# An encoder trunk in fp32 on one core: latents copied out of their banks, squares taken chunk by chunk, taps booked by the number of chunks under way, a warm-up activation in the join

## The chip, the core and the metric

The kernel runs on one core of a Trainium2 chip. The metric is the device time of one execution in microseconds: 1187.85 us, the median of three runs (1186.94 to 1188.17). The profiled execution took 1188.38 us.

## What is computed

A two-layer encoder on x of 512 positions and 1024 channels, in float32. Each sub-layer is `x = x + rms_norm(f(rms_norm(x)))`.

```python
def parallel_conv_mla(h, ...):        # layer 0
    proj = h @ w_in                   # gates and input of a 3-tap convolution, q_lat (384), kv_lat (256), k_rope
    y_a = gate_b * depthwise_conv(gate_c * xs, sc_kernel)
    q = rms_norm(q_lat, q_norm) @ w_uq
    kv = rms_norm(kv_lat, kv_norm) @ w_ukv
    ...
    y_b = block_attention(q_full, k_full, v)
    return jnp.concatenate([y_a, y_b], axis=-1) @ w_out

def conformer_conv(h, ...):           # layer 1
    u = h @ w_pw1 + b_pw1
    a, g = jnp.split(u, 2, axis=-1)
    u = a * jax.nn.sigmoid(g)
    u = depthwise_conv(u, w_dw) + b_dw          # 31 taps per channel
    u = jax.nn.silu(layer_norm(u, ln_g, ln_b))
    return u @ w_pw2 + b_pw2

def squared_relu_mlp(h, w1, w2):      # both layers, hidden width 4096
    return jnp.square(jax.nn.relu(h @ w1)) @ w2
```

## The kernel before

Everything is held transposed: channels in eight chunks of 128 partitions, positions along the free axis. A float32 product is made of three matmuls on pairs of a high and a low part (`mm`, L242 to L248). `strip` (L210) loads a strip of weights of 128 x 1024, lets ACT round it to the high part (`whi`, L223) and GpSimd subtract to the low part (`wlo`, L224); `split` (L227) does the same for activations, on ACT (L230) and mostly on VectorE (L233, L236, L238). So one strip is 24 matmuls in one PSUM bank. The eight banks are named by use: S (three), pj (two), mi (two) and o (one). `scratch` (L174) takes o and mi in turn, and under a norm or join also pj.

The start (L557 to L609). `split_x` loads a chunk of x, multiplies it by its gain into a scratch bank (L569) and splits it into a pair h. `START` says between which chunks the first two strips of `win` are loaded. After all eight chunks, each is squared (`Sum.square`, L357, into a scratch bank) and added up on VectorE (`Sum.add`, L332). `Sum.done` adds over partitions with small matmuls (L367), `rstd` works out 1/sqrt on VectorE in some twelve small instructions (L390 to L425), and `spread` brings the result back to all partitions with matmuls (L432). ACT copies it out as R0 (L595). `latent` (L598) makes five latents, each a strip's product, multiplied by R0 in its own bank (L603), squared for its norm, and split from there.

The second part (`M2`, L36) is a program written out by hand: steps of the two halves A and B of the positions. While the chain of one half runs (a norm, a join), `hold` and `pace` pull steps of the other half in (`step`, L293), until the next step of the same half or the next chain. The 31 taps of the convolution run on VectorE (`convolve`, L813; L827), each adding into the chunk's bank in place. Chunks stand in `convs` as generators; `fill(us)` (L276) adds us to a credit after every matmul step and issues taps of the first two chunks in turn as long as the credit covers the cost of a tap, which is `TAP_US` by the width of the half. `norm_step` (L927) first issues the taps that are left, pulling a step for each `STEP_US - OP_US` of them, and then runs `layer_norm`, which ends in the pairs h that `pw2` multiplies. `up_step` (L885) lets ACT take the square of the relu as long as taps are left, and VectorE after that.

VectorE's order in this part is the order of the code. The other engines' order, and all orders of the first part, are set by a scheduler at build time, which may place an instruction wherever its operands are ready. `warm` is a 1-element tile on which an activation is called only to have a function's table loaded (L847, silu).

Of the kernel before, what the change touches and what calls it, by code (L numbers as in the profile page):

```python
# [12 lines left out]
AF = mybir.ActivationFunctionType  # L13
# [4 lines left out]
T = 512  # L18
# [18 lines left out]
M3 = [('up', 'B', 1, 3, 0, 8), ('down', 'B', 1, 3, 0, 8), ('finish', 'B')]  # L37


OP_US, STEP_US = 0.39, 2.35  # L40
TAP_US = {T // 2 - PAD: 0.41, T // 2 + PAD: 0.44}
FILL = {'up': 2.3, 'down': 2.3, 'first': 2.6, 'sum': 1.8, 'pw1': 4.8, 'pw2': 2.3}
START = ['x', (128,), 'x', (256, 512, 768), 'x', 'x', 'x', 'x', 'x', 'x', ()]
ADD0 = 0
# [87 lines left out]
def trunk(ctx: ExitStack, tc: tile.TileContext, a, out: bass.AP):  # L132
# [11 lines left out]
    def new(pool, tag, bufs, w=T, dt=F32):  # L144
        uid[0] += 1
        return pool.tile([P, w], dt, tag=tag, bufs=bufs, name=f"{tag}{uid[0]}")
# [46 lines left out]
    def small(w=NB):  # L193
        return new(sp, f"s{w}", 8 if w == 1 else 12, w)
# [77 lines left out]
    def settle(keep=0):  # L272
        while len(late) > keep:
            late.pop(0)()

    def fill(us):  # L276
        if scope.get("pulling"):
            return
        credit[0] += us
        while convs:  # L280
            turn[0] += 1
            conv, cost = convs[turn[0] % min(len(convs), 2)]
            if credit[0] < cost:
                break
            credit[0] -= cost
            if next(conv, None) is None:
                convs.remove((conv, cost))
        if not convs:
            credit[0] = min(credit[0], 0.0)

# [85 lines left out]
    def rstds(total, ratio=None):  # L376

        hold()
        r = rstd(total.done(), D, ratio)
        hold()  # L380
        return spread(r, total.seg)
# [75 lines left out]
    def join(xs, ms, s, post, pre, hs, seg, h, mlp):  # L457
# [33 lines left out]
        if mlp:  # L491
# [5 lines left out]
            lack[h] = ratios(h, seg, ssq)  # L497
            return
        bc = rstds(ssq)
        for j in range(NC):  # L500
            t = scratch(seg.w)
            nc.vector.scalar_tensor_tensor(
                out=t, in0=xs[j][seg.sl], scalar=col(pre + j), in1=bc, op0=ALU.mult, op1=ALU.mult
            )
            settle()
            split((hv[j][0][seg.sl], hv[j][1][seg.sl]), t, nc.vector, late=late)
            pace(2)
# [46 lines left out]
        ycat=("ycat", 4 * NB, T), sqf=("ycat", 4 * NB, T), acc1f=("ycat", 4 * NB, T),  # L554
        pt=("pt", 4, 2 * T), pr=("pr", 4, T + 2), tq=("tq", 1, T),
    )
    warm = small(1)  # L557
    nc.vector.memset(warm, 0.0)
    nc.scalar.activation(warm, warm, AF.Copy)
    nc.sync.dma_start(vec[:, :V_QN], a["vecs"][:, :V_QN])  # L560
    xs = [Win(xt()) for _ in range(NC)]
    hs = [hpair() for _ in range(NC)]
# [3 lines left out]
    def split_x(j):  # L566
        load_x(xs[j], j)
        t, (hi, lo) = scratch(T), (h.t[:, :T] for h in hs[j])
        nc.vector.tensor_scalar(out=t, in0=xs[j].t, scalar1=col(gains(0, 0) + j), scalar2=None, op0=ALU.mult)  # L569
        settle()  # L570
        split((hi, lo), t, nc.vector, late=late)

    win, j = [], 0
    for what in START:
# [5 lines left out]
    nc.sync.dma_start(kst, a["consts"])  # L580
    nc.sync.dma_start(vec[:, V_QN:], a["vecs"][:, V_QN:])
    settle()
    for j in range(NC):
        s0.square(xs[j].t)
        settle()

    def spread_sb(r):
        t = xt()
# [9 lines left out]
    def latent(m0, n, gain, slot):  # L598
        lat, ss = [], Sum(n, FULL, whole=WL)
        for j in range(n):  # L600
            acc = linear(win[m0 + j] if m0 + j < len(win) else strip(a["win"][m0 + j]), hs)
            t = acc
            nc.vector.tensor_tensor(out=t, in0=acc, in1=R0, op=ALU.mult)  # L603
            ss.square(t)
            settle()
            h = slot(), slot()
            split((h[0].t, h[1].t), t, nc.vector, col(gain + j))
            lat.append(h)
        return lat, lambda: rstd(ss.done(), n * P)  # L609
# [227 lines left out]
    def layer_norm(seg):  # L837
# [6 lines left out]
        )  # L844
        hold()
        total = spread(mu, seg)
        nc.scalar.activation(warm, warm, AF.Silu)  # L847
        s2 = Sum(NC, seg, whole=WHOLE[2])
        for c in range(NC):
            v = vs[c][:, seg.sl]  # L850
# [26 lines left out]
                convolve(*todo.pop(0))  # L877


    hid, sums, kept, us, lack = {}, {}, {}, [], {}  # L880

    def seg_of(h, layer):
        return {"A": (A, A2), "B": (B, B2), "F": (FULL, FULL)}[h][layer]
# [147 lines left out]
    )  # L1031
    us.extend(tmp("u") for _ in range(NC))

    warm = new(sp, "warm", 1, 1)
    nc.vector.memset(warm, 0.0)
    vs = [m.t for m in ms]
    run(M2)
    ph.__exit__(None, None, None)
# [109 lines left out]
```

## Time and profile before

| what | value |
|---|---|
| median of three runs | 1187.85 us (1186.94 to 1188.17) |
| profiled execution | 1188.38 us, its span 1186.6 us |
| PE busy | 1142.9 us, 96% of the span |
| POOL (GpSimd) busy | 845.4 us |
| ACT busy | 664.6 us |
| DVE (VectorE) busy | 648.3 us |
| mean granted clock of PE | 0.986 |

Times are in us from the start of the span. PE is the matrix engine, PEld its weight loads. "PEclk" or "clock" is the share of the full clock that the chip granted PE: 1.00 is 2.4 GHz, 0.50 is 1.2 GHz. An arrow in a wait points from the waiting instruction to the one that ended the wait. `out<-in` are names of tiles; L223 is line 223.

### The profile page before, as it was taken

To read this page: it belongs to the slowest core of one execution; us is meant where nothing else is said; L and a number is where in the kernel's file an instruction comes from. 1 tells how busy PE (TensorE), PEld (TensorE's weight loads), DVE (VectorE), ACT (ScalarE), POOL (GpSimd) and SP (SyncE) were. 2 spreads that over 40 slices of the span, in tenths; PEclk is the share of its full clock that TensorE was granted. 3 is DMA by queue.
4 is the path that set the end of the run, shared out by engine and by line. 5 is a ranking of instruction groups with operands and counts; after the bars stand their busy time and mean duration, and the time that the engine had idled before them with its cause. 6 is when DMAs were issued, how large, how long until landed. Compare 5 with 4: busy or idle time off the path is not lost.

```text
span 1186.6 us, 22844 instructions
## 1 busy us (share of the span) xinstructions
PE 1142.9 (96%) x8850; PEld 1102.7 (93%) x8850; DVE 648.3 (55%) x1699; ACT 664.6 (56%) x1217; POOL 845.4 (71%) x409
## 2 busy tenths in 40 slices
PE   7899989999999999899999999999997999999995
PEld 6688878999999999899999999999997999999995
DVE  5642699554522125499984275599995273222123
ACT  6421577556845457545466677546456685544352
POOL 5654554148988888698877778688886777878681
PEclk9899999999999999999999999999999999999998
DMA  6411332027655555465554555465555455553441
GB/s 210 160 59 36 94 116 72 1 91 243 205 178 194 181 178 194 126 208 183 185 190 160 178 177 179 149 195 194 195 186 168 143 172 177 187 183 134 137 148 38
DMA packets 55404, 183.99 MB, mean 155 GB/s; under 512 B 6400, under 2 KB 10880, under 8 KB 55296
## 3 DMA queue, kind: packets, MB, share of 16 engines
q1 hardware_dynamic: 54720, 181.86, 46.6%
q8 instruction: 69, 1.13, 0.4%
q10 hardware_dynamic: 576, 0.68, 0.2%
q14 instruction: 39, 0.32, 0.1%
HBM read 180.42 MB, written 2.10 MB: 154 GB/s over the span
## 4 chain that ended last, share of the span: by engine, by line
PE 86%; DVE 6%; ACT 4%; DMA 2%; POOL 1%; issue 1%; SPq 0%; POOLq 0%; ACTq 0%; DVEq 0%
PE S L246 22%; PE S L247 21%; PE S L248 21%; PE pj L246 6%; PE pj L247 6%; PE pj L248 6%; ACT whi L223 2%; DVE pr L762 1%; DMA raw<-in_win 1%; POOL wlo L224 1%; DVE s L756 1%; PE mi L432 1%; PE mi L367 1%; DVE pt L236 1%; PE mi L765 1%
## 5 line engine op out<-in xcount | busy, mean ns | idle before, releaser
L224 POOL TENSOR_TENSOR wlo<-raw,whi 128x1024 fp32r<-128x1024 f32 (+2 forms) x347 | 802.4, 2325 | 268.7 <-ACT whi L223 260.8
L223 ACT ACTIVATE whi<-raw 128x1024 fp32r<-128x1024 f32 (+2 forms) x347 | 355.9, 1030 | 391.1 <-PE S L247 200.0
L246 PE MATMUL S<-h,whi 128*128 128x256 f32 (+3 forms) x1208 | 348.2, 291 | 11.8 <-DVE u L804 4.6
L247 PE MATMUL S<-h,whi 128*128 128x256 f32 (+3 forms) x1208 | 349.1, 290 | 0.1
L248 PE MATMUL S<-h,wlo 128*128 128x256 f32 (+3 forms) x1208 | 349.1, 290 | 0.0
L246 PEld LDWEIGHTS S<-h,whi 128*128 128x128 f32 x1208 | 228.4, 191 | 18.3 <-ACT h L230 5.2
L246 PE MATMUL S<-hid,whi 128*128 128x256 f32 (+2 forms) x840 | 234.8, 282 | 2.3 <-DVE acc L332 2.1
L247 PE MATMUL S<-hid,whi 128*128 128x256 f32 (+2 forms) x840 | 235.5, 281 | 0.0
L248 PE MATMUL S<-hid,wlo 128*128 128x256 f32 (+2 forms) x840 | 234.8, 280 | 0.0
L247 PEld LDWEIGHTS S<-h,whi 128*128 128x128 f32 x1208 | 229.7, 190 | 3.8 <-DVE h L233 0.5
L248 PEld LDWEIGHTS S<-h,wlo 128*128 128x128 f32 x1208 | 229.6, 190 | 3.7 <-POOL wlo L224 0.2
L827 DVE SCALAR_TENSOR_TENSOR pj<-u,taps,pj 128x240 f32<-128x240 f32 (+1 forms) x464 | 195.3, 485 | 2.0
L246 PEld LDWEIGHTS S<-hid,whi 128*128 128x128 f32 x840 | 157.8, 189 | 3.7 <-DVE acc L332 2.9
L248 PEld LDWEIGHTS S<-hid,wlo 128*128 128x128 f32 x840 | 158.6, 189 | 0.0
L247 PEld LDWEIGHTS S<-hid,whi 128*128 128x128 f32 x840 | 158.5, 189 | 0.1
L246 PE MATMUL pj<-h,whi 128*128 128x272 f32 (+3 forms) x344 | 107.7, 313 | 10.1 <-ACT h L230 5.5
L247 PE MATMUL pj<-h,whi 128*128 128x272 f32 (+3 forms) x344 | 107.6, 313 | 0.0
L248 PE MATMUL pj<-h,wlo 128*128 128x272 f32 (+3 forms) x344 | 106.5, 309 | 0.0
L246 PEld LDWEIGHTS pj<-h,whi 128*128 128x128 f32 x344 | 66.4, 193 | 13.7 <-ACT h L230 5.8
L247 PEld LDWEIGHTS pj<-h,whi 128*128 128x128 f32 x344 | 66.5, 193 | 3.9 <-DVE h L233 0.9
L248 PEld LDWEIGHTS pj<-h,wlo 128*128 128x128 f32 x344 | 66.5, 193 | 3.3 <-issue 0.2
L236 DVE TENSOR_TENSOR hid<-S,hid 128x256 fp32r<-128x256 f32 (+2 forms) x102 | 42.8, 421 | 47.8 <-ACT hid L230 47.2
(250 smaller groups left out, 1629.6 us busy)
## 6 DMA issues: line engine op xcount, KB each, us to landing
raw<-in_w SPq DMA_DIRECT2D x256, 512.0 KB, 3.3
raw<-in_pw SPq DMA_DIRECT2D x48, 512.0 KB, 3.3
raw<-in_win SPq DMA_DIRECT2D x16, 512.0 KB, 3.3
x<-in_xT SPq DMA_DIRECT2D x16, 256.0 KB, 4.4
raw<-in_wout SPq DMA_DIRECT2D x8, 512.0 KB, 3.3
raw<-in_wq SPq DMA_DIRECT2D x8, 192.0 KB, 2.4
out<-x SPq DMA_DIRECT2D x8, 120.0 KB, 2.5
out<-x SPq DMA_DIRECT2D x5, 136.0 KB, 1.7
```

The source lines that it names most:

```text
L223: nc.scalar.activation(h, r, AF.Copy)
L224: nc.gpsimd.tensor_tensor(out=lo[:, c0:c1], in0=r, in1=h.bitcast(F32), op=ALU.subtract)
L236: eng.tensor_tensor(out=lo, in0=src, in1=hi.bitcast(F32), op=ALU.subtract)
L246: nc.tensor.matmul(acc, sh, mh, start=i == 0, stop=False)
L247: nc.tensor.matmul(acc, sh, ml, start=False, stop=False)
L248: nc.tensor.matmul(acc, sl, mh, start=False, stop=i == n - 1)
L367: nc.tensor.matmul(s[:, b : b + 1], q[:, sl.start - self.seg.lo : sl.stop - self.seg.lo], one, start=i == 0, stop=i == len(self.parts) - 1,)
L432: nc.tensor.matmul(o[:, sl], r[:, b : b + 1].to_broadcast([bw, P]), ident[:bw, :bw], start=True, stop=True,)
L756: nc.vector.reduce_max(out=mx, in_=S, axis=AX.X)
L762: eng.tensor_scalar(out=pr_, in0=pr_, scalar1=sm, scalar2=None, op0=ALU.mult)
L765: nc.tensor.transpose(tp[:, kb * P : (kb + 1) * P], pr_[:, kb * P : (kb + 1) * P], ident)
L827: nc.vector.scalar_tensor_tensor(out=dst, in0=src, scalar=wk, in1=acc, op0=ALU.mult, op1=ALU.add)
```

## The change

`latent` writes its product to a tile of its own in SBUF (tag ycat, as the sums' tiles) and not back into its bank. Each chunk's square is issued in `split_x`, right behind that chunk's split, and no longer after all eight. `TAP_US` has two costs for each width, and `fill` takes the second when one chunk alone is under way. The join that does not lead into an MLP calls a sigmoid on `warm` between its second norm and its scaling; for that `warm` becomes a list that is filled before M2.

```diff
-TAP_US = {T // 2 - PAD: 0.41, T // 2 + PAD: 0.44}
+TAP_US = {T // 2 - PAD: (0.385, 0.51), T // 2 + PAD: (0.41, 0.54)}
...
-            conv, cost = convs[turn[0] % min(len(convs), 2)]
+            conv, costs = convs[turn[0] % min(len(convs), 2)]
+            cost = costs[len(convs) == 1]
             if credit[0] < cost:
                 break
             credit[0] -= cost
             if next(conv, None) is None:
-                convs.remove((conv, cost))
+                convs.remove((conv, costs))
...
         bc = rstds(ssq)
+        nc.scalar.activation(warm[0], warm[0], AF.Sigmoid)
         for j in range(NC):
             t = scratch(seg.w)
...
-    warm = small(1)
-    nc.vector.memset(warm, 0.0)
-    nc.scalar.activation(warm, warm, AF.Copy)
+    first = small(1)
+    nc.vector.memset(first, 0.0)
+    nc.scalar.activation(first, first, AF.Copy)
...
         split((hi, lo), t, nc.vector, late=late)
+        s0.square(xs[j].t)
...
     settle()
-    for j in range(NC):
-        s0.square(xs[j].t)
-        settle()
...
             acc = linear(win[m0 + j] if m0 + j < len(win) else strip(a["win"][m0 + j]), hs)
-            t = acc
+            t = tmp("ycat")
             nc.vector.tensor_tensor(out=t, in0=acc, in1=R0, op=ALU.mult)
...
-        nc.scalar.activation(warm, warm, AF.Silu)
+        nc.scalar.activation(warm[0], warm[0], AF.Silu)
...
-    warm = new(sp, "warm", 1, 1)
-    nc.vector.memset(warm, 0.0)
+    warm.append(new(sp, "warm", 1, 1))
+    nc.vector.memset(warm[0], 0.0)
```

The lines of the changed file are one to three higher (L223 is L224, L332 is L334, L357 is L359, L847 is L848). ACT's first instructions (`whi` is a strip's high part, `h` a chunk's, `ycat` and `mi` from `x` are squares) before:

```order
L559 ACT_TABLE_LOAD
L559 ACTIVATE s_75<-s_75 128x1
L847 ACT_TABLE_LOAD
L847 ACTIVATE warm_2832<-warm_2832 128x1 x2
L357 ACTIVATE ycat_175<-x_79 128x512
L223 ACTIVATE whi_108<-raw_107 128x128
L230 ACTIVATE h_87<-mi_104 128x512
```

and of the change:

```order
L562 ACT_TABLE_LOAD
L562 ACTIVATE s_75<-s_75 128x1
L502 ACT_TABLE_LOAD
L502 ACTIVATE warm_2837<-warm_2837 128x1
L848 ACT_TABLE_LOAD
L848 ACTIVATE warm_2837<-warm_2837 128x1
L502 ACT_TABLE_LOAD
L502 ACTIVATE warm_2837<-warm_2837 128x1
L848 ACT_TABLE_LOAD
L848 ACTIVATE warm_2837<-warm_2837 128x1
L359 ACTIVATE ycat_107<-x_79 128x512
```

The two sigmoids of the joins and the two silus of the norms stand at the head of the program, in turn, each with a load; before, two silus stood there behind one load.

VectorE in the start (L569 or L572 is a chunk's product with its gain, L233 or L234 the low part of its split, L332 or L334 the sum of squares), behind the first two chunks before:

```order
L569 TENSOR_SCALAR mi_137<-x_81,vec 128x512
L569 TENSOR_SCALAR o_142<-x_82,vec 128x512
L569 TENSOR_SCALAR mi_147<-x_83,vec 128x512
L233 TENSOR_TENSOR h_92<-mi_137,h_91 128x512
L233 TENSOR_TENSOR h_94<-o_142,h_93 128x512
L569 TENSOR_SCALAR mi_157<-x_85,vec 128x512
L233 TENSOR_TENSOR h_96<-mi_147,h_95 128x512
```

and of the change:

```order
L572 TENSOR_SCALAR o_141<-x_81,vec 128x512
L334 TENSOR_TENSOR ycat_107<-ycat_107,mi_146 128x512
L334 TENSOR_TENSOR ycat_107<-ycat_107,mi_154 128x512
L234 TENSOR_TENSOR h_92<-o_141,h_91 128x512
L334 TENSOR_TENSOR ycat_107<-ycat_107,mi_162 128x512
L572 TENSOR_SCALAR o_149<-x_82,vec 128x512
L334 TENSOR_TENSOR ycat_107<-ycat_107,mi_170 128x512
L334 TENSOR_TENSOR ycat_107<-ycat_107,mi_178 128x512
L234 TENSOR_TENSOR h_94<-o_149,h_93 128x512
L572 TENSOR_SCALAR o_157<-x_83,vec 128x512
L334 TENSOR_TENSOR ycat_107<-ycat_107,mi_186 128x512
```

The products of all chunks but the first now go to the one bank o, each behind the split of the chunk before it, and the squares' sums stand between them; the last of them stands ahead of the fourth chunk's split on, not behind the eighth's.

PE around the second sum of norm B (L367 or L369 is the sum, L432 or L434 its spread; matmuls of 128x240 are up steps of half A, those of 128x272 are pw2, which reads the norm's result) before:

```order
L248 MATMUL S_11702<-h_2190,wlo_11502 128x240
L367 MATMUL mi_11637<-kst,acc_11487 128x1 x3
L432 MATMUL mi_11692<-kst,s_11642 128x128 x3
L246 MATMUL S_11812<-h_2176,whi_11602 128x272
L246 MATMUL S_11879<-h_2176,whi_11697 128x272
```

and of the change:

```order
L249 MATMUL S_11601<-h_2195,wlo_11413 128x240
L369 MATMUL mi_11524<-kst,acc_11398 128x1 x3
L247 MATMUL S_11655<-h_2181,whi_11456 128x240
...
L249 MATMUL S_11655<-h_2195,wlo_11457 128x240
L434 MATMUL mi_11575<-kst,s_11529 128x128 x3
L247 MATMUL S_11706<-h_2181,whi_11493 128x240
...
L249 MATMUL S_11749<-h_2195,wlo_11545 128x240
L247 MATMUL S_11819<-h_2181,whi_11650 128x272
```

One up step of 24 matmuls now stands between the sum and its spread, and two behind the spread, where before there was none; the norm begins three steps earlier among PE's matmuls. At norm A it begins two steps earlier, and four up steps stand behind the spread of its second sum, where two stood.

## Rows read from the trace of the kernel before

**Rows 1.** Part 1 of the page: busy time of each engine, its share of the span, and its instructions.

```profile
PE 1142.9 (96%) x8850; PEld 1102.7 (93%) x8850; DVE 648.3 (55%) x1699; ACT 664.6 (56%) x1217; POOL 845.4 (71%) x409
```

**Rows 2.** Busy time by stretches of the start. Columns: the stretch, its length, then busy us and records of PE, PEld, DVE, ACT and POOL, the granted clock of PE, the share of the DMA engines and GB/s.

```profile
5.46:13.25 7.79, 7.26 (x15) 4.49 (x16) 5.91 (x9) 4.63 (x9) 4.87 (x5) 1.00 1.02 369
13.25:40.20 26.95, 26.95 (x129) 22.24 (x127) 11.17 (x28) 13.48 (x18) 17.19 (x8) 1.00 0.45 150
40.20:44.76 4.56, 0.01 (x2) 0.00 (x1) 3.89 (x7) 3.56 (x6) 3.80 (x2) 0.91 0.54 194
44.76:50.80 6.04, 6.04 (x14) 4.78 (x15) 5.09 (x8) 5.41 (x9) 3.46 (x3) 0.50 0.50 163
```

**Rows 3.** The timeline of PE at 10 us: start, busy us, engine, line, operation, tiles.

```profile
10.54 0.63 PE L248 MATMUL S<-h,wlo 128*128 128x512 f32 x1
10.97 0.63 PE L246 MATMUL S<-h,whi 128*128 128x512 f32 x1
```

**Rows 4.** Groups of PE's instructions from 13.25 to 40.2, shapes kept apart: the two that are not part of a strip's product. Columns: count, busy us, mean ns of one, idle time before.

```profile
L367 PE MATMUL mi<-kst,ycat 128*128 128x1 f32 x14 | 1.6, 244 | 0.0
L432 PE MATMUL mi<-kst,s 128*128 128x128 f32 x8 | 1.1, 275 | 0.0
```

**Rows 5.** The timeline from 40 to 54 us: R0, the first product by it, PE's first matmul after its stop, and the small sum behind the sixth strip. In brackets the idle time ahead of it on its engine and what ended it.

```profile
40.24 0.60 ACT L595 ACTIVATE R<-mi 128x512 f32<-128x512 f32 x1 [0.50 <-PE mi L432]
40.87 0.70 DVE L603 TENSOR_TENSOR pj<-pj,R 128x512 f32<-128x512 f32 x1 [6.19 <-ACT R L595]
...
44.76 0.79 PE L246 MATMUL pj<-h,whi 128*128 128x512 f32 x1 [4.55 <-DVE x L238]
...
53.16 0.95 PE L367 MATMUL mi<-kst,ycat 128*128 128x1 f32 x8
```

**Rows 6.** Busy time by stretches at norm A, norm B and under the taps; columns as in group 2.

```profile
650.00:654.00 4.00, 2.50 (x13) 1.55 (x12) 2.06 (x6) 4.00 (x11) 3.38 (x2) 1.00 0.23 56
654.00:660.00 6.00, 6.00 (x40) 6.00 (x41) 1.88 (x6) 3.05 (x8) 1.65 (x2) 0.72 0.42 140
902.00:914.00 12.00, 7.77 (x66) 7.39 (x65) 8.00 (x29) 9.50 (x21) 8.62 (x4) 1.00 0.43 141
914.00:922.00 8.00, 6.04 (x30) 5.85 (x30) 6.12 (x16) 6.66 (x16) 0.00 (x0) 0.57 0.20 68
...
535.00:625.00 90.00, 90.00 (x765) 90.00 (x764) 79.47 (x207) 50.93 (x83) 74.32 (x32) 1.00 0.56 182
775.00:890.00 115.00, 115.00 (x1016) 115.00 (x1015) 108.24 (x263) 63.18 (x99) 100.31 (x42) 1.00 0.58 191
```

**Rows 7.** What PE waited for at the first sigmoid of pw1 (450 to 535 us) and at norm B (890 to 925 us): us in total, times, longest.

```profile
PE S L246 <- DVE u L804: 2.4, 2, 2.2
...
PE mi L432 <- DVE s L418: 2.4, 1, 2.4
PE S L246 <- ACT h L230: 2.0, 1, 2.0
```

**Rows 8.** The timeline of ACT at the start: the second table load, the warm-ups, the first square, the first strip's and the first chunk's high part.

```profile
2.25 1.28 ACT L847 ACT_TABLE_LOAD   x1
3.54 0.44 ACT L847 ACTIVATE warm<-warm 128x1 f32<-128x1 f32 x2
3.95 0.63 ACT L357 ACTIVATE ycat<-x 128x512 f32<-128x512 f32 x1
4.48 0.29 ACT L223 ACTIVATE whi<-raw 128x128 fp32r<-128x128 f32 x1
4.82 0.60 ACT L230 ACTIVATE h<-mi 128x512 fp32r<-128x512 f32 x1
```

**Rows 9.** Groups of the first 45 us on DVE (a product with the gain, a split, an add of squares) and POOL (a strip's low part); columns as in group 4.

```profile
L569 DVE TENSOR_SCALAR o<-x,vec 128x512 f32<-128x512 f32 x4 | 3.0, 752 | 1.0 <-DMA x<-in_xT 1.0
L233 DVE TENSOR_TENSOR h<-o,h 128x512 fp32r<-128x512 f32 x4 | 2.8, 689 | 2.1 <-ACT h L230 2.1
L332 DVE TENSOR_TENSOR ycat<-ycat,mi 128x512 f32<-128x512 f32 x4 | 2.7, 687 | 0.1
...
L224 POOL TENSOR_TENSOR wlo<-raw,whi 128x1024 fp32r<-128x1024 f32 x9 | 21.5, 2390 | 11.5 <-ACT whi L223 11.5
```

**Rows 10.** Groups of DVE: taps of half A with two chunks under way (538 to 553 us); taps of half B with two, and the eviction of an up step (800.3 to 815.2 us); taps of the last chunk of half B alone (883 to 891 us). Columns as in group 4; busy us is the time that the group covers, so taps that overlap count once.

```profile
L827 DVE SCALAR_TENSOR_TENSOR pj<-u,taps,pj 128x240 f32<-128x240 f32 x33 | 12.6, 467 | 0.0
...
L827 DVE SCALAR_TENSOR_TENSOR pj<-u,taps,pj 128x272 f32<-128x272 f32 x31 | 13.1, 502 | 0.0
L236 DVE TENSOR_TENSOR hid<-S,hid 128x240 fp32r<-128x240 f32 x4 | 1.6, 405 | 0.9 <-ACT hid L230 0.9
...
L827 DVE SCALAR_TENSOR_TENSOR pj<-u,taps,pj 128x272 f32<-128x272 f32 x13 | 6.6, 504 | 0.4
```

**Rows 11.** The timeline at norm B: the second sum, its spread, and the last low part of the norm's result.

```profile
910.14 0.73 PE L367 MATMUL mi<-kst,acc 128*128 128x1 f32 x6
...
913.30 0.91 PE L432 MATMUL mi<-kst,s 128*128 128x128 f32 x6 [2.43 <-DVE s L418]
...
921.50 0.44 DVE L233 TENSOR_TENSOR h<-o,h 128x272 fp32r<-128x272 f32 x1 [0.46 <-ACT h L230]
```

**Rows 12.** Groups of ACT from 899 to 922 us: a strip's high part, and one of an up step; columns as in group 4.

```profile
L223 ACT ACTIVATE whi<-raw 128x1024 fp32r<-128x1024 f32 x4 | 4.2, 1058 | 4.5 <-PE S L247 3.3 <-POOL wlo L224 1.1
...
L230 ACT ACTIVATE hid<-S 128x240 fp32r<-128x240 f32 x4 | 1.5, 364 | 0.0
```

More of the change, by code (lines that the diff above doesn't have):

```diff
@@ L877, in start @@
                 convolve(*todo.pop(0))
-    hid, sums, kept, us, lack = {}, {}, {}, [], {}
+    hid, sums, kept, us, lack, warm = {}, {}, {}, [], {}, []
     def seg_of(h, layer):
```

## The prediction

> **What bounds the kernel now.** I read the page first: PE is busy 1142.9 of 1186.6 us [rows 1], so at most 44 us of idle PE and what a halved clock takes can be won. The edits touch four stretches, and I cut the trace there. In the start PE issues its first matmuls slowly: 15 records in the 7.79 us to 13.25, then 129 in 26.95 us [rows 2]. Matmuls of 512 columns come 0.43 us apart at first (10.54, 10.97 [rows 3]); after 13.25 they come (26.95 - 1.6 - 1.1) / 107 = 0.227 apart [rows 2, 4]. The first is the 1.2 GHz level, the second 2.4, though the clock column prints 1.00 for both stretches; at 44.76 it prints 0.50 for the same 6.04 / 14 = 0.43 [rows 2]. At 40.2 PE stops for 4.55 us: five latents stand in all five S and pj banks, and none leaves before R0 is there (ACT at 40.24, DVE's first multiply by it at 40.87, in place in the bank, which is held until its split ends). After the stop 6.04 us run at 0.50 [rows 2, 5]. That is 4.55 + 3.02 = 7.6 us lost.
>
> The two layer norms are the next places. At norm A (650 to 660) PE is idle 1.50 us and runs 6.0 us at a mean clock of 0.72, which is 1.7 more: 3.2 us. At norm B (902 to 922) it is idle 4.23 + 1.96 us and its 6.04 busy us at 0.57 cost 2.6: 8.8 us [rows 6]. What it waits for there is the norm's own chain: DVE s L418, then ACT h L230 [rows 7]. In the stretches of the taps (535 to 625, 775 to 890) PE is never idle, while DVE is busy 88% and 94% [rows 6].
>
> **Tables.** The change asks for the sigmoid's table inside the join. On ACT the order shows that the little activation does not stay there: with the other warm-ups it stands at the head of the program, as the old ones did, and four loads alternate where one stood. A load takes 1.28 us; with its activation it is 1.29 (2.25 to 3.54) + 0.22, about 1.51 [rows 8]. So ACT's first square moves from 3.95 to 2.25 + 4 x 1.51 = 8.3 us, **4.35 us later**, with nothing ahead of it to hide that. Both loads before the sigmoids of pw1 stay, so the PE wait of 2.2 us behind the first sigmoid [rows 7] stays. The Trainium skill, page "ScalarE: Activation LUTs", section "What ACT_TABLE_LOAD costs", counts a drain of some 1.38 us behind each load. The trace disagrees: the activation starts 1.29 us after its load, so there is no room for a drain [rows 8]. By the page three more loads would cost about 4.1 us more (an estimate from it), and the kernel would take some 1181 us.
>
> **Start.** Squares and the single bank: with a scratch taken for each square, the chunks' products all fall into o, one bank, and the squares into the two of mi. On DVE the order shows the chain: add, split, product, in turn. The first split ends on ACT at 8.3 + 0.53 + 0.34 + 0.60 = 9.8 (the steps 3.95, 4.48, 4.82 [rows 8]). From there DVE runs 15 instructions to the last add: four splits of 0.69, four products of 0.75, seven adds of 0.69 [rows 9], 10.6 us, so it ends at 20.4. In PE's order the sum of squares (14 small matmuls, 1.6 us) stands behind 26 matmuls of the first four chunks; at 0.43 each those fit into the time until about 21. PE then goes on at about 22.5 (20.4, the 1.6 [rows 4] and a hop). From there 92 matmuls finish the five latents, then come the spread of R0, the next small sums and the sixth strip's 24: 116 x 0.227 + 1.1 + 0.95 = 28.4 [rows 4, 5], so the sixth strip and that sum are done at 50.9. Before, that sum ends at 53.16 + 0.95 = 54.1 [rows 5]. Gain **3.2 us**; I take 3.0. R0's copy stands on ACT behind the last chunk's split (about 28) and two strips' whi, so it is there at about 35, ahead of the 44 at which the sixth strip needs a bank. So the stop at 40 goes, by the early squares and not by the extra tile: writing the latents to ycat only shortens a hold that then no longer ends last. Weights keep ahead: the splits of 2.39 us on POOL [rows 9] are faster than the 24 x 0.227 = 5.4 us that PE needs for a strip. Bounds: gain 5 (nothing but the 4.35 us moves PE, less what was slow there anyway), loss 3 (30 further matmuls at 0.43 instead of 0.227, twice as many as the 14 at 44.76 [rows 2]).
>
> **Taps.** Two chunks under way cost 12.6 / 33 = 0.38 us a tap of 240 and 13.1 / 31 = 0.42 of 272; one alone costs 6.6 / 13 = 0.51 of 272 [rows 10]. The new table says 0.385 and 0.41, 0.51 and 0.54, so it books what the trace shows. In a step of 24 matmuls (24 x 90.0 / 765 = 2.82 us, 24 x 115.0 / 1016 = 2.72 [rows 6]) DVE now gets 2.3 us of taps and one eviction of 0.40 [rows 10]: 2.70, just under both. So I cost the denser taps at nothing, under PE's matmuls; if DVE fell behind, the split of hid would come late for the next matmuls. What it moves is the end of the taps: the sum before norm A stands 52 PE rows earlier in the order, that before norm B 74, about two and three steps. These steps are then left to be pulled in under the norm.
>
> **Norm A.** Behind the spread of the second sum PE has 96 matmuls before its first of pw2, 48 before. The 48 more are 48 x 0.118 = 5.7 us against 3.2 us lost [rows 6]: I take 3.0. Bounds 1 and 3.2: the extra up steps also put their relu, square and split on ACT.
>
> **Norm B.** PE stood 2.4 us between the sum and its spread, and 2.0 between the spread and the first h [rows 7]. Now 24 matmuls (2.7 us) stand in the first gap: the chain there runs from 910.14 to 913.30, 3.16 us with the 0.73 of the sum itself [rows 11], so it closes. In the second stand 48, 5.4 us. The last h ended 921.94 - 913.30 = 8.6 us after the spread began [rows 11]. Among the eight silus and splits now stand two whi (1.06) and five short ones of up steps (0.36) [rows 12]: 3.9 us, so 12.5. PE offers the spread's 0.9, 5.4, and some 35 matmuls of pw2, wider by 272/240 and so 0.13 each, that it can do on the first h: 10.9. About 2 us of idle remain, and about 2 for a clock that halves after it, as it did after the 1.50 us at norm A [rows 6]. 8.8 - 4.0 = **4.8 us**. Bounds 2.5 (ACT's queue holds the h back) and 8.8.
>
> **Sum.** 3.0 + 3.0 + 4.8 = 10.8 us. The profiled execution's own time is 1188.38 (its span of 1186.6 and 1.8 around it), which gives 1177.6; the median of the runs is 0.5 lower, so **1177 us**.
>
> **Rivals.**
> - Everything at norm B hides: 8.8 instead of 4.8 there, 1173 us. For it speaks that the sum's half (squares behind down steps, which need no ACT) gets quicker too; against it ACT, which has no idle time there. 0.15.
> - The norms are bound by their own chain on ACT: gains of 1 and 2.5 stand, 3.0 + 3.5 = 6.5, 1181.5 us. For it: at 650 to 654 ACT is busy all 4.00 us [rows 6]. 0.12.
> - The start eats itself: DVE's chain of 15 has a wait in each hop and the sum reaches PE some 4 us later. 7.8 - 1 = 6.8, 1181 us. 0.11.
> - Each table load holds ACT for longer than its one row shows: at twice the 1.29 us [rows 8] the three more cost 3.9 us more, 1181 us; against it stands that row. 0.02. The drain that the page "ScalarE: Activation LUTs" of the Trainium skill counts would be such a wait.
> - The slow norms and the slow start together: 3.5 - 1 = 2.5, 1185.5 us, at the edge of 0.2% (2.4 us, about what a measurement of this kernel tells from no change), so I count it as no change. 0.08.
> - **The clock stays low in the start.** PE gets its first matmuls with gaps until the sum of squares at 20 to 22 us, and if the 1.2 GHz level holds, each matmul of 512 takes 0.20 more. Against 10.8 us the point is 54 matmuls beyond the 26; for all 92 it is 18.4 us: 1177 + 18.4 = 1195 us. For it: at 44.76 six dense us ran at 0.50 after a stop [rows 2]. Against it: in the start of before the spacing fell to 0.227 at 13.25 although PE had been fed with gaps [rows 2, 4]. The Trainium skill, page "TensorE: Matmul & The Clock Gate", section "Part 1: The HAM clock gate", says that the slow state is the default and activity lifts it; the trace agrees in both places. 0.06.
> - That the change does nothing can be excluded for order and taps by the order itself; for the sigmoid's table it is my forecast.
>
> **How the numbers follow.** Forecast 0.46; faster by over 0.2%: 0.46 + 0.15 + 0.12 + 0.11 + 0.02 = 0.86; within: 0.08; slower: 0.06. The range goes from 1170 (start 5, norms 3.2 and 8.8: 17 us) to 1186, which takes in both mishaps together and leaves out the low clock.
>
> **What would show it.** Five table loads within the first 8.3 us of ACT and the first square there; the first R0 multiply by about 36 us and no PE stop at 40; the sixth strip's sum near 51; two loads at the sigmoids unchanged; no PE idle in 535 to 625 and 775 to 890; PE idle and half clock gone at norm A and about halved at norm B. Wrong if the 512-column matmuls are still 0.43 apart after 23 us, if PE waits for DVE hid among the taps, or if R0 comes after 44.

## The result, and the profile after

The changed kernel takes **1179.68 us**, the median of four runs (1178.15 to 1180.92); the kernel before took 1187.91 beside it. The ratio is 0.9932 (95% interval 0.9914 to 0.9949): 8.2 us faster, well beyond what can't be told from no change. The forecast was 1177, a gain of 10.8. The profiled execution took 1179.89 us, its span is 1178.1.

PE's busy time fell by 5.5 us and its idle time by 3, as part 1 of the page shows beside [rows 1]:

```profile
PE 1137.4 (97%) x8850; PEld 1097.8 (93%) x8850; DVE 649.9 (55%) x1702; ACT 668.1 (57%) x1219; POOL 846.9 (72%) x409
```

The matmuls are the same in number and width, so the 5.5 us are clock, not work: the mean granted clock went from 0.986 to 0.991. Where the time went is read from PE's small sums (L369) and spreads (L434). Ahead of the seven in this table, PE's order holds the same number of matmuls in all kernels shown here (one more at the second of them in e7_banks), and by the shapes in the traces the same columns, so a difference at one of them is time won or lost by then. Each row is one execution, and the clock differs between executions of one kernel as well: of the kernel before, timed beside e5 to e7, one run took 1184.34 us at a mean granted clock of 0.990 and another 1188.49 at 0.986. A us or two of a row can be that execution's own. The first row gives their times in the kernel before; the others, how much **earlier** each comes (us; profiled executions).

| kernel | end of start | end of attention | first join | after norm A | second join | after norm B | last sum |
|---|---|---|---|---|---|---|---|
| before, at | 122.07 | 298.43 | 483.36 | 683.21 | 747.35 | 947.12 | 1173.75 |
| the change | 3.32 | 4.45 | 4.44 | 6.76 | 6.77 | 8.52 | 8.55 |
| e1_taps | 0.23 | 1.65 | 1.64 | 5.38 | 5.38 | 6.66 | 6.37 |
| e2_squares | 6.36 | 7.86 | 7.85 | 6.78 | 6.78 | 6.85 | 6.50 |
| e3_latents | 5.79 | 7.32 | 7.31 | 7.35 | 7.34 | 7.32 | 7.30 |
| e4_no_sigmoid | 6.24 | 7.76 | 7.75 | 11.50 | 11.48 | 12.72 | 12.64 |
| e5_held | 5.33 | 6.69 | 6.68 | 9.50 | 9.51 | 14.80 | 14.53 |
| e6_vec_squares | 6.33 | 7.83 | 7.83 | 10.02 | 10.04 | 10.98 | 11.32 |
| e7_banks | -0.39 | -0.49 | -0.39 | 3.35 | 3.37 | 4.59 | 4.88 |
| e8_late | 6.01 | 5.97 | 5.95 | 12.12 | 12.11 | 19.65 | 19.96 |
| e9_late_no_silu | 5.57 | 5.62 | 5.60 | 10.74 | 10.74 | 14.41 | 14.40 |

The change's own row: 3.32 in the start, 1.13 in the attention, 2.32 between the joins (norm A and the first sigmoid of pw1), 1.75 behind the second join (the second sigmoid and norm B). For the last two the forecast had 7.8 and they gave 4.1.

**ACT's head** in the changed kernel, from its timeline (start, busy us, engine, line, operation); it answers to [rows 8]:

```profile
0.73 1.28 ACT L562 ACT_TABLE_LOAD   x1 [0.73 <-PEq L1137]
2.25 1.28 ACT L502 ACT_TABLE_LOAD   x1
3.76 1.28 ACT L848 ACT_TABLE_LOAD   x1
5.28 1.28 ACT L502 ACT_TABLE_LOAD   x1
6.79 1.28 ACT L848 ACT_TABLE_LOAD   x1
8.09 0.20 ACT L848 ACTIVATE warm<-warm 128x1 f32<-128x1 f32 x1
8.20 0.61 ACT L359 ACTIVATE ycat<-x 128x512 f32<-128x512 f32 x1
```

Five loads, and the first square at 8.20 (forecast 8.3).

**The start**, from the timelines of the changed kernel: the last add of squares, their sum on PE, R0, the first multiply by it, the next small sum (now ahead of the sixth strip), and the first matmul behind that strip. They answer to [rows 4, 5]:

```profile
19.38 0.68 DVE L334 TENSOR_TENSOR ycat<-ycat,mi 128x512 f32<-128x512 f32 x1
20.11 1.61 PE L369 MATMUL mi<-kst,ycat 128*128 128x1 f32 x13
...
34.72 0.58 ACT L596 ACTIVATE R<-mi 128x512 f32<-128x512 f32 x1
35.33 0.69 DVE L604 TENSOR_TENSOR ycat<-pj,R 128x512 f32<-128x512 f32 x1 [6.73 <-ACT R L596]
44.32 0.95 PE L369 MATMUL mi<-kst,ycat 128*128 128x1 f32 x8
50.74 0.39 PE L247 MATMUL S<-h,whi 128*128 128x512 f32 x1
```

DVE's chain ends at 20.06, R0 is there at 35, and the sixth strip is done at 50.74: forecast 20.4, 35 and 50.9.

**Stretches** of the changed kernel (columns as in [rows 2]): the start from 22 us on, the former stop at 40, the taps of both halves, norm A, norm B up to the second spread, behind it, and its end; last the 4.55 us behind the first sigmoid's stop. They answer to [rows 2, 6]:

```profile
22.00:44.32 22.32, 22.32 (x103) 18.35 (x101) 13.78 (x29) 12.73 (x18) 14.98 (x7) 1.00 0.46 150
40.00:51.00 11.00, 11.00 (x54) 9.13 (x53) 10.61 (x16) 5.97 (x8) 8.85 (x4) 1.00 0.45 138
535.00:595.00 60.00, 60.00 (x510) 60.00 (x510) 56.82 (x153) 32.08 (x50) 50.80 (x22) 1.00 0.55 187
765.00:875.00 110.00, 110.00 (x969) 110.00 (x969) 107.74 (x267) 61.77 (x100) 94.81 (x41) 1.00 0.57 193
640.00:650.00 10.00, 8.34 (x71) 8.14 (x70) 5.65 (x16) 9.15 (x22) 6.89 (x4) 1.00 0.48 159
878.00:898.40 20.40, 19.15 (x169) 18.79 (x168) 9.39 (x34) 10.02 (x17) 17.22 (x8) 1.00 0.58 201
898.40:909.45 11.05, 8.54 (x69) 7.74 (x68) 4.75 (x15) 10.81 (x23) 6.68 (x4) 1.00 0.38 124
909.45:914.00 4.55, 4.46 (x21) 4.26 (x22) 2.95 (x8) 2.37 (x6) 0.80 (x1) 0.62 0.47 169
...
497.45:502.00 4.55, 4.55 (x26) 4.55 (x27) 4.22 (x10) 1.76 (x4) 4.55 (x3) 0.65 0.70 232
```

No PE stop at 40 any more. Under the taps PE is never idle though DVE is now busy 95% and 98%. At norm A 1.66 us of idle are left and the clock holds; at norm B 1.25 ahead of the second spread, and behind it 2.5 idle us in which ACT is busy 10.81 of 11.05, then a lower clock (0.62).

**Norm B**, the timeline of PE's stops in the changed kernel, and of ACT behind the spread of 898.44 [rows 7, 11, 12]:

```profile
888.61 0.38 PE L247 MATMUL S<-hid,whi 128*128 128x240 f32 x1 [0.49 <-DVE m L535]
892.33 0.35 PE L247 MATMUL S<-h,whi 128*128 128x240 f32 x1 [0.76 <-DVE m L535]
...
905.41 0.36 PE L247 MATMUL S<-h,whi 128*128 128x272 f32 x1 [0.76 <-ACT h L231]
908.14 0.39 PE L247 MATMUL S<-h,whi 128*128 128x272 f32 x1 [1.34 <-ACT h L231]
909.45 0.39 PE L247 MATMUL S<-h,whi 128*128 128x272 f32 x1 [0.32 <-ACT h L231]
```

```profile
898.58 1.06 ACT L224 ACTIVATE whi<-raw 128x1024 fp32r<-128x1024 f32 x1 [1.23 <-PE S L248]
899.54 0.35 ACT L521 ACTIVATE y<-S 128x240 f32<-128x240 f32 x1
899.93 0.38 ACT L523 ACTIVATE S<-y 128x240 f32<-128x240 f32 x1
900.32 1.28 ACT L863 ACT_TABLE_LOAD   x1
901.62 0.58 ACT L863 ACTIVATE pj<-m,vec 128x272 f32<-128x272 f32 x1
...
911.18 0.40 ACT L231 ACTIVATE h<-o 128x272 fp32r<-128x272 f32 x1
```

ACT works without a gap from 898.58 to 911.58. The work of an up step that was pulled in, and the load of silu's table, stand between the spread and the first silu, which comes 3.18 us behind the spread (901.62 - 898.44). In the kernel before the load ran from 912.42 to 913.70, mostly ahead of the spread at 913.30, and the first silu came at 914.71, 1.41 behind it.

### The profile page after: what moved, and what is told of

It is laid out like the page before. It is cut to its first block, busy times and chain, and to the rows that moved or that the text cites. A ratio compares the mean times of both kernels' runs of the same rounds, so it can differ in the third digit from the quotient of the medians.

```text
span 1178.1 us, 22855 instructions
## 1 busy us (share of the span) xinstructions
PE 1137.4 (97%) x8850; PEld 1097.8 (93%) x8850; DVE 649.9 (55%) x1702; ACT 668.1 (57%) x1219; POOL 846.9 (72%) x409
## 3 DMA queue, kind: packets, MB, share of 16 engines
q8 instruction: 69, 1.13, 0.4%
## 4 chain that ended last, share of the span: by engine, by line
PE 87%; DVE 5%; ACT 5%; issue 1%; POOL 1%; DMA 0%; POOLq 0%; ACTq 0%; DVEq 0%
PE S L247 22%; PE S L248 22%; PE S L249 21%; PE pj L247 6%; PE pj L248 6%; PE pj L249 6%; ACT whi L224 1%; DVE pr L763 1%; PE mi L369 1%; DVE s L757 1%; PE mi L434 1%; DVE pt L237 1%; POOL wlo L225 1%; PE mi L766 0%; PE o L248 0%
## 5 line engine op out<-in xcount | busy, mean ns | idle before, releaser
L224 ACT ACTIVATE whi<-raw 128x1024 fp32r<-128x1024 f32 (+2 forms) x347 | 355.8, 1030 | 381.3 <-PE S L248 189.8
L828 DVE SCALAR_TENSOR_TENSOR pj<-u,taps,pj 128x240 f32<-128x240 f32 (+1 forms) x464 | 191.7, 483 | 1.1
L247 PE MATMUL pj<-h,whi 128*128 128x272 f32 (+3 forms) x344 | 106.8, 310 | 11.7 <-ACT h L231 9.7
L248 PE MATMUL pj<-h,whi 128*128 128x272 f32 (+3 forms) x344 | 105.8, 308 | 0.0
```

What stands on the lines that cost most here:

```text
L224: nc.scalar.activation(h, r, AF.Copy)
L247: nc.tensor.matmul(acc, sh, mh, start=i == 0, stop=False)
L248: nc.tensor.matmul(acc, sh, ml, start=False, stop=False)
L828: nc.vector.scalar_tensor_tensor(out=dst, in0=src, scalar=wk, in1=acc, op0=ALU.mult, op1=ALU.add)
```

## The experiments

All were timed against the kernel before, in five rounds; it took 1187.04 us beside e1 to e4, 1187.41 beside e5 to e7 and 1188.58 beside e8 and e9. The expectations are absolute times, mostly built on 1187.9 or on the change's 1179.7, so between kernels of different sets about a us is open.

### e1_taps: the taps' new costs alone

```diff
 # on the kernel before
-TAP_US = {T // 2 - PAD: 0.41, T // 2 + PAD: 0.44}
+TAP_US = {T // 2 - PAD: (0.385, 0.51), T // 2 + PAD: (0.41, 0.54)}
...
-            conv, cost = convs[turn[0] % min(len(convs), 2)]
+            conv, costs = convs[turn[0] % min(len(convs), 2)]
+            cost = costs[len(convs) == 1]
```

> The kernel before with the new costs of the taps alone (TAP_US and fill). Account by stretches: of the 8.2 us of the whole change, norm A gave 3.2 and norm B 1.9, and the stop at the first sigmoid, which is 2.21 us long in both, cost 0.9 more because the clock fell behind it. So 1187.9 - 5.1 = 1182.8 us if the clock stays up behind that stop, 1183.7 if it falls there again. Rival, the sizes of the forecast: 3.0 + 4.8, 1180.1 us. Rival, the norms' gain comes from where the start ended and not from the taps: 1187.9 us.

1182.66 us, ratio 0.9966 (0.9953 to 0.9978): the first value, to 0.2 us, though against the kernel before beside it the gain is 4.4 us and not 5.1. In the profiled executions 3.74 us are won between the joins and 1.28 behind the second (the table above). The clock held behind the first sigmoid's stop; the 1.4 us by which that stretch of the change stands behind (2.32 against 3.74) are that fall of the clock. Not all of the 3.74 us is norm A. In the kernel before, PE also waited at 508.00 and at 634.19, outside the norm, for VectorE; the profile counts 0.18 us of idle at each, but by the starts of the matmuls each cost 0.44 us (0.46 and 0.22 us to the next start, where 0.12 is usual). Neither wait is there in e1 or in the change, which leaves about 2.8 us for the norm itself. The first of them, in the kernel before:

```profile
508.00 0.38 PE L246 MATMUL S<-h,whi 128*128 128x256 f32 x1 [0.18 <-DVE u L804]
```

And the stop of the start is untouched, 4.46 us at 45.89.

### e2_squares and e3_latents: the two edits of the start, each alone

```diff
 # e2_squares, on the kernel before
         split((hi, lo), t, nc.vector, late=late)
+        s0.square(xs[j].t)
...
-    for j in range(NC):
-        s0.square(xs[j].t)
-        settle()
 # e3_latents, on the kernel before
-            t = acc
+            t = tmp("ycat")
```

> The kernel before with the squares behind each chunk alone: two table loads at the head instead of five, all else of the start as in the change. Theory: DVE's chain of 15 instructions and the small sum behind it set the start, and the three more loads move that chain as a whole, so the sixth strip's sum, at 50.65 in the change and 53.2 to 54.1 before, comes 4.35 earlier, at 46.3: 1187.9 - 3.4 - 4.35 = 1180.1 us. Rival: the arrival of x and of the weights, or the slow matmuls, set the start, and the loads were hidden: 1184.5 us, the sum at 50.6. No PE stop at 40 in either; if the stop of 4.5 us is there, it went by the latents' tile.

1181.89 us, 0.9955 (0.9941 to 0.9968). No PE stop at 40, R0 at 31.70; at the end of the start 6.36 us are won, 3 more than in the change, which has three more loads. The time lies between the two expectations because the clock fell behind the first sigmoid's stop here too (7.85 at the first join, 6.78 behind norm A).

> The kernel before with the latents written to a tile in SBUF alone. Theory: a latent is held in its bank until R0 is there, whichever tile it is then written to, so the stop of 4.55 us at 40.2 stays and the time with it: 1187.9 us, at most 0.7 us less because the bank is free one multiply earlier. Rival: the bank held until the split is what stops PE: the stop shrinks to under 2 us, and the half clock with it, 1183 us.

1181.10 us, 0.9953 (0.9941 to 0.9966). **My theory falls.** PE's stop in this kernel, and the multiply that ends it:

```profile
41.20 0.50 PE L246 MATMUL pj<-h,whi 128*128 128x512 f32 x1 [1.41 <-DVE ycat L603]
```

```profile
40.45 0.69 DVE L603 TENSOR_TENSOR ycat<-pj,R 128x512 f32<-128x512 f32 x1 [6.19 <-ACT R L595]
```

R0 comes hardly earlier than before (the multiply at 40.45 against 40.87 in [rows 5]), and yet the stop is 1.41 instead of 4.55 us and the clock stays up: the bank is free when the multiply has read it, and no longer when the square and the split have. What I had set at 0.7 us at most is 3.1 us and the clock behind it.

### e4_no_sigmoid: the change without the warm-up that was hoisted

```diff
         bc = rstds(ssq)
-        nc.scalar.activation(warm[0], warm[0], AF.Sigmoid)
```

> The changed kernel without the sigmoid in the join: ACT's head has two table loads instead of five. Theory: its start is one chain from ACT's first square on, 4.35 us earlier: 1179.7 - 4.35 = 1175.3 us, the sixth strip's sum at 46.3 instead of 50.65, and both stops at the sigmoids of pw1 still 2.2 us, since the load stands there in either kernel. Rival: the loads were hidden behind the arrival of x and of the weights, 1179.7 us. Rival: the sigmoid does something in the join after all, and its stops grow: above 1179.7 us.

1176.60 us, 0.9914 (0.9900 to 0.9928). The three extra loads cost 2.9 us at the end of the start, not 4.35 (the medians lie 3.1 us apart, or 2.2 when each is set against the kernel before beside it). With two loads, the start waits for transfers, as ACT's second high part and VectorE's second product show in this kernel's timeline:

```profile
6.41 0.95 ACT L224 ACTIVATE whi<-raw 128x896 fp32r<-128x896 f32 x1 [1.01 <-DMA raw<-in_win]
...
7.29 0.76 DVE L571 TENSOR_SCALAR o<-x,vec 128x512 f32<-128x512 f32 x1 [1.16 <-DMA x<-in_xT]
```

In the change these waits lie under the loads. Both sigmoids still stop PE (2.21 us each). Next to e2 and e3 this also says that the two edits of the start do not add up: 6.24 with both, 6.36 and 5.79 with one.

### e5_held: the warm-ups tied to their places by data

```diff
         bc = rstds(ssq)
-        nc.scalar.activation(warm[0], warm[0], AF.Sigmoid)
+        nc.scalar.activation(warm[0], bc[:, :1], AF.Sigmoid)
...
         total = spread(mu, seg)
-        nc.scalar.activation(warm[0], warm[0], AF.Silu)
+        nc.scalar.activation(warm[0], total[:, :1], AF.Silu)
```

> The changed kernel with both warm-ups tied to their place by data: the sigmoid reads the join's spread bc, the silu the norm's spread of the mean, so neither can be moved ahead of them; ACT's head keeps one load. Theory: against the change without the sigmoid (1176.6 us, two loads at the head) one load less in the start gains 1.3 us; the load no longer stands ahead of the sigmoids of pw1, so their two stops of 2.21 us shrink to about 0.9 and the clock falls less behind the second (1.3 each, and 1.3 of clock); at the norms it no longer stands between the spread and the first silu: the 1.66 us of idle at norm A fall to about 0.4 and norm B gains 1.3. 1176.6 - 1.3 - 2.6 - 1.3 - 1.3 - 1.3 = 1169 us. Rival: the load in the join holds up the eight h that pw1 waits for by 1.5 us, and PE stops there: about 1173 us. Rival: sine gets a load of its own, which PE waits for: 1.3 us more than either.

1173.59 us, 0.9889 (0.9876 to 0.9902): the first rival's value. The 1.3 us expected in the start did not come (5.33 won at its end, 6.24 in e4): sine now has a table load of its own (54.60, L634), as the second rival had it, though PE shows no wait there. PE and ACT around the first join and its sigmoid:

```profile
480.61 1.01 PE L247 MATMUL S<-h,whi 128*128 128x256 f32 x3 [3.33 <-ACT h L231]
497.16 0.39 PE L247 MATMUL S<-h,whi 128*128 128x256 f32 x1 [0.78 <-DVE u L805]
```

```profile
478.16 1.28 ACT L502 ACT_TABLE_LOAD   x1
480.18 0.38 ACT L231 ACTIVATE h<-o 128x256 fp32r<-128x256 f32 x1 [0.56 <-DVE o L505]
```

The sigmoid's stop shrinks to 0.78 as expected, but the load stands ahead of the first h that pw1 needs, and PE stops there for 3.33 us. Behind the second join the kernel wins 5.29 us where e4 won 1.24: the sigmoid's stop, and the load taken out of ACT's queue at norm B.

### e6_vec_squares: three squares off ACT under norm B

```diff
 # on e4_no_sigmoid; in up_step and norm_step
-        scope["square"] = nc.scalar if convs or todo or scope.get("pulling") else nc.vector
+        scope["square"] = nc.scalar if convs or todo or scope.get("pulling") and not scope.get("nb") else nc.vector
...
+        scope["nb"] = h == "B"
         layer_norm(seg_of(h, 1))
+        scope["nb"] = False
```

> The changed kernel without the sigmoid in the join, and the three up steps pulled in under norm B take the square of their relu on VectorE instead of ACT (three instructions of 0.38 us). Theory: at norm B ACT's queue holds the h back (13 us without a gap from the spread to the last h), so the last h comes 0.8 to 1.1 us earlier and PE's loss behind the spread falls by as much, more where the clock then stays up: 1176.6 - 1.0 = 1175.6 us, and in the trace PE's idle time at norm B down from 2.6 to about 1.5. Rival: VectorE or the banks bind there, and the idle time stays at 2.6: 1176.6 us or up to 1 more.

1176.95 us, 0.9916 (0.9902 to 0.9930), the same as e4; its stretch behind the second join is 0.3 us worse (0.94 against 1.24 won). PE's one stop behind the spread:

```profile
904.61 0.59 PE L247 MATMUL S<-h,whi 128*128 128x272 f32 x1 [3.26 <-DVE hid L237]
```

That low part of hid (an up step's result) frees the bank that PE waits for, and it had itself waited for ACT, as VectorE's timeline shows:

```profile
904.15 0.41 DVE L237 TENSOR_TENSOR hid<-S,hid 128x240 fp32r<-128x240 f32 x1 [1.78 <-ACT hid L231]
```

ACT is without a gap from 896.88 to 904.12, silu's load first. VectorE had that step's square done at 902.37, and ACT came to its split only at 903.72, behind a whi, a relu and an h. So the rival's time came, with stops of 3.26 us behind the spread where e4 has 2.13, but the bank still comes free by way of ACT's queue. e8 and e9 show more directly what an instruction in ACT's queue costs at norm B.

### e7_banks: the chunks' products in two banks

```diff
 # on e4_no_sigmoid: the squares go to SBUF, the products to o and mi in turn
-        s0.square(xs[j].t)
+        s0.square(xs[j].t, tmp("sqf"))
```

> The changed kernel without the sigmoid in the join, the squares of x in SBUF tiles of their own, so that the chunks' products take o and mi in turn again and not the one bank o. Theory: the chain of VectorE through one bank sets when the later chunks reach PE; with two banks the matmuls of the first five strips come sooner after the small sum, but the sum itself keeps its 15 instructions of VectorE, so the sixth strip's work moves by under 1 us: 1176 us. Rival: the one bank costs what the order suggests, a wait in each of six hops, 2 to 3 us: 1174 us. Rival: squares in SBUF reach the sum later, R0 with them: 1178 us.

1179.86 us, 0.9943 (0.9926 to 0.9960): the last rival, and 1.9 us more. In the profiled execution the sum of squares starts at 26.14 instead of 17.18, R0 at 36.80 instead of 32.16, and the next root (`rstd`'s small instructions on VectorE) is late for the sum behind it:

```profile
60.85 1.33 PE L369 MATMUL mi<-kst,ycat 128*128 128x1 f32 x8 [1.93 <-DVE s L420]
```

The clock is 0.61 in the eight us behind this stop, and at the end of the start all that the two edits had won is gone (-0.39). That execution took 1183.52 us and was the slowest of six (1177.65 to 1183.52); the medians of e7 and e4 lie 3.3 us apart.

The run does not price the one bank, because the squares' tiles brought in something else. An add of squares now reads two tiles in SBUF. Four of the seven took about 0.7 us, as all seven do in e4, where one of the two operands is in a bank; the other three took 2.16, 1.63 and 2.77 us. Each of these three began 0.5 to 1.5 us into a subtraction on GpSimd and ended 0.55 us behind that subtraction's end (9.88, 18.93, 21.73). The last two of them, and GpSimd's two:

```profile
17.84 4.44 DVE L334 TENSOR_TENSOR ycat<-ycat,ycat 128x512 f32<-128x512 f32 x2
16.39 5.33 POOL L225 TENSOR_TENSOR wlo<-raw,whi 128x1024 fp32r<-128x1024 f32 x2 [2.84 <-ACT whi L224]
```

They lengthen VectorE's chain by 4.5 us; the sum comes 9 us later. What two banks would give with the squares left in banks was not run.

### e8_late and e9_late_no_silu: the sigmoid's load behind the last h

```diff
 # e8_late, on e5_held: behind the join's loop instead of ahead of it
-        nc.scalar.activation(warm[0], bc[:, :1], AF.Sigmoid)
...
         settle()
+        nc.scalar.activation(warm[0], hv[NC - 1][0][seg.sl][:, :1].bitcast(F32), AF.Sigmoid)
 # e9_late_no_silu, on e8_late
-        nc.scalar.activation(warm[0], total[:, :1], AF.Silu)
```

> As the warm-ups held by data (1173.6 us), but the sigmoid's reads the last h of the join's loop instead of its spread, so its table load stands behind the eight h. Theory: there the load ahead of the h made PE idle 2.72 us instead of 1.18 at the first join, and the clock fell behind that (1.6 us); both go, and the stops at the sigmoids stay at 0.78: 1173.6 - 1.5 - 1.6 = 1170.5 us, down to 1170 if the second join loses its 0.3 too. Rival: behind the h the load holds up the high parts of pw1's strips, and through them GpSimd and PE: 1172 to 1174 us.

**1168.07 us**, 0.9829 (0.9816 to 0.9843): 20.5 us faster than before, 11.6 faster than the change. PE's stops at the first join, its sigmoid and norm B, and the load on ACT:

```profile
479.20 0.61 PE L247 MATMUL S<-h,whi 128*128 128x256 f32 x3 [1.19 <-ACT h L231]
494.53 0.39 PE L247 MATMUL S<-h,whi 128*128 128x256 f32 x1 [0.79 <-DVE u L805]
...
898.58 0.39 PE L247 MATMUL S<-h,whi 128*128 128x272 f32 x1 [0.96 <-ACT h L231]
```

```profile
484.57 0.39 ACT L231 ACTIVATE h<-pj 128x256 fp32r<-128x256 f32 x1 [0.89 <-DVE pj L504]
484.97 1.28 ACT L511 ACT_TABLE_LOAD   x1
486.27 0.20 ACT L511 ACTIVATE warm<-h 128x1 f32<-128x1 f32 x1
489.11 1.06 ACT L224 ACTIVATE whi<-raw 128x1024 fp32r<-128x1024 f32 x1 [2.64 <-issue]
```

Behind the h ACT has nothing to do until 489, and the load costs nothing. The stop at the first join is 1.19 us against 3.33 in e5. The clock is 1.00 at both sigmoids and at both norms. That is where most of the two us beyond the expectation come from: behind the second join e8 won 7.54 us and e5 5.29, where 0.3 was expected at most. The stops at norm B are as long in e5 (0.95 and 0.32 us), but there the clock fell behind them (0.91 over 890 to 910 us), and here it did not; this much of the gain was not foretold.

> As the run with the sigmoid behind the join's last h, but with no silu warm-up at all: its load stands between the spread and the first silu again at both norms. Theory: ACT's queue sets the norms' ends, so idle time at norm A goes back from 0.65 to 1.66 us, and norm B loses 1.9 us more (0.8 idle, the rest clock): 1170.5 + 1.0 + 1.9 = 1173.4 us. Rival: at the norms the matmuls pulled in hide the load, and the gain there in the run before came from elsewhere: 1170.5 us.

1173.55 us, 0.9877 (0.9864 to 0.9891): the expected time, but not the expected difference. It was to be 2.9 us above e8, and e8 itself came 2.4 us below its expectation, so leaving out silu's warm-up cost 5.5 us. With silu's load back in the queue, norm A's idle time is 1.66 us again (0.64 in e8), and at norm B PE's stops and the clock (two stretches, 890 to 910 us, of this kernel; of e8 the second line) are:

```profile
898.60 0.36 PE L247 MATMUL S<-h,whi 128*128 128x272 f32 x1 [0.76 <-ACT h L231]
901.33 0.39 PE L247 MATMUL S<-h,whi 128*128 128x272 f32 x1 [1.38 <-ACT h L231]
```

```profile
890.00:910.00 20.00, 17.77 (x119) 16.68 (x118) 9.08 (x29) 14.15 (x31) 9.08 (x4) 0.83 0.36 123
```

```profile
890.00:910.00 20.00, 18.55 (x148) 17.70 (x148) 8.36 (x23) 16.36 (x35) 11.16 (x6) 1.00 0.33 108
```

One load of 1.28 us in ACT's queue there is 0.8 us of idle PE plus a sixth of the clock over 20 us: 3.9 us between the two kernels behind the second join (7.54 against 3.67 won), where 1.9 were expected. Between the joins it is 1.0 (6.17 against 5.14), as expected.

## Why the prediction was right, and where it failed

The sign, the size within 2.7 us and the places were right: what the change itself gave lies in the start and at the two norms. The order was not: norm B was to give most and gave least. Two things that no term had, 1.1 us won in the attention and 1.4 lost to a fall of the clock, nearly cancel; that the sum is not further off by either is luck.

- **Tables: right as to the order, the cost too high.** The five loads stand in the first 8.1 us, the loads at both sigmoids stay, and so do their stops of 2.2 us. "Nothing ahead of it to hide that" was wrong by 1.4 us: without the loads the start waits for x and the first strip (e4), which [rows 9] already show as a wait for DMA. The rival of longer loads is out: three loads with their activations cost less than 4.35 us, not more.
- **Start: right in size, wrong in one cause.** 20.06 for the chain's end (20.4), 35.3 for the first multiply (about 36), 50.7 for the sixth strip (50.9); 3.3 us against 3.0. From 22 us on PE ran at the 2.4 GHz level (103 records in 22.32 us), so the rival of the low clock and that of DVE's hops are out. But the sentence that the stop at 40 goes "by the early squares and not by the extra tile" is wrong: e3 shows that the tile alone takes 3.1 of its 4.55 us and the low clock behind it. Each of the two edits does the work of both.
- **Taps: right.** No PE idle under them, at 95% and 98% of DVE.
- **Norm A: right.** 3.74 between the joins in e1, of which 0.9 are the two waits for VectorE outside the norm, which the forecast did not have; about 2.8 are left for the norm (forecast 3.0, bounds 1 and 3.2). In the change 1.4 went again behind the first sigmoid, in another stretch: there the clock fell to 0.65 behind the same 2.21 us stop that left it at 1.00 in the kernel before.
- **Norm B: the term that was mis-sized, 1.75 instead of 4.8** (below its lower bound of 2.5), 1.28 in e1. Up to the second spread 2.7 us were won: the spread comes 14.86 us earlier (913.30 to 898.44), of which 48 x 0.113 = 5.4 (169 records in 19.15 us) are the 48 matmuls of 240 columns that it has fewer ahead of it, and 6.77 were there at the second join. I had taken the whole 4.23 for the wait for the root, which is 2.43 of it [rows 7, 11]; that wait did close. The other 1.8 were two waits for VectorE of an up and a down step (0.96 <-DVE hid L236, 0.85 <-DVE m L532, at 907.38 and 903.50 in the kernel before), and such stops stay in the change: two, for a bank that a down step's add (DVE m L535) has still to read, 1.25 us. Behind the spread I had counted on 0.6 gained, and 0.9 was lost. ACT's last h ends 13.1 us behind the spread and its low part on VectorE 13.6, where I had 12.5 and where it was 8.6 before: each step pulled in puts a whi, a relu, a square and a split there, 2.2 us (1.06 + 0.35 + 0.38 + 0.37) for the 2.7 us of matmuls that it gives PE, so by these rows a step covers only about half a microsecond (an estimate). And silu's load, which ended beside the spread before, moved into the chain. Its place was there to be read in ACT's order; I counted instructions, not the load.
- **The attention's 1.1 us were not in the forecast, and I don't put them down to the change.** The stops there are of nearly the same length (3.5 us before, 3.3 in the change and in e1); in the profile of before the clock fell to 0.83 behind them (160 to 170 us). In e1, whose start is the one of before, it did not, and 1.4 us are won there too.

So the sum by steps is 3.3 + 3.7 - 1.4 + 1.75 + 1.1 = 8.5 us in the profiled executions, against 3.0 + 3.0 + 4.8. The rival that the norms are bound by their own chain on ACT (6.5 us in all) holds for norm B, where even its 2.5 us was too much, and not for norm A.

The Trainium skill, page "ScalarE: Activation LUTs", section "What ACT_TABLE_LOAD costs", counts a drain of about 1.38 us with each load. Here the activation starts 1.30 us after the start of its load, which takes 1.28 (6.79 to 8.09, 484.97 to 486.27, 900.32 to 901.62), and the loads at the head follow each other every 1.51 us with an activation between them, so there is no room for it.

## What to carry to other kernels

A warm-up activation on a constant tile is not where it is written: a scheduler may put all of them at the head, where each can cost a load in the start and warm nothing, as the two sigmoids did here. Let it read a value that is produced where it should stand, and choose that place behind the last urgent instruction of ACT, not ahead of the first; here that took the changed kernel from 1179.7 to 1168.1 us, more than the whole change had won. When work is pulled in under a chain to cover it, count what that work puts on the engine of the chain itself, table loads included: the cover is the difference. Of two edits that free the same bank, measure each alone before a gain is put down to one of them. And when an edit moves an operand to another memory, look at the time of each instruction that reads it before the result is put down to the banks (e7).

## What the runs showed that was not expected

- The same stop of 2.21 us at the first sigmoid left PE's clock at 1.00 in the kernel before, e1, e3, e4 and e7, and was followed by a lower one in the change (0.65 over 4.55 us), e2 and e6; behind the second sigmoid, with the same stop, it fell in every kernel that had it. Behind stops of 0.8 us there it stayed up (e5, e8, e9). These are one execution of each kernel, and what decides at 2.2 us stays open. The Trainium skill, page "TensorE: Matmul & The Clock Gate", section "Part 1: The HAM clock gate", calls the moment at which the clock rises in a kernel's start variable from run to run; no run here shows whether the falls behind these stops vary in that way. The fall at the first sigmoid is worth 1.4 us, which no count of instructions foretells.
- PE keeps its pace under taps that fill DVE to 98%: 969 matmuls in 110 us, 1016 in 115 before at 94%.
- Three adds on VectorE that read two tiles in SBUF took 1.6 to 2.8 us instead of 0.7, each ending 0.55 us behind a GpSimd subtraction that was running when it began (e7).
